# Attention of block 1: units that take the heads of both partition halves, with alternating products

## The chip, the cores and the metric

The kernel runs on one core of a Trainium2 chip. The metric is the device time of one execution in microseconds (us), lower is better; a time is the median of several runs. Engines are named as in the profile: PE (TensorE matmuls), PEld (its weight loads), DVE (VectorE), ACT (ScalarE), POOL (GpSimd), SP (the DMA queue used most).

## What is computed

The program is two blocks of a network on 512 tokens of width 1024. Block 1 projects its normalised input to many streams, runs a windowed attention in three groups of 8 heads of width 64 on some of them and a gated recurrence on others, and merges both. Block 2 (not touched here) has more attention, a second recurrence and two layers of experts. What matters is the attention of block 1, per group with dilation 1, 4 or 16:

```
s = jnp.einsum('bnqrhd,bnkrhd->bnrhqk', qb, kh) + bias
s = jnp.where(valid[None, :, None, None], s, NEG_INF)
m = jnp.max(s, axis=-1, keepdims=True)
p = jnp.exp(s - m)
den = jnp.transpose(jnp.sum(p, axis=-1), (0, 1, 4, 2, 3))
o = jnp.einsum('bnrhqk,bnkrhd->bnqrhd', p, vh) / den[..., None]
```

Queries see keys at most 64 positions away in their group's order; blocks out of range are masked. The outputs of the three groups are then mixed by their maxima and sums.

## The kernel before

`attention1` is the second stage of block 1. It first builds Q, K and V of the three groups with `matrix`: projections as triples of matmuls in split precision (lines 102 to 104, 128x512, called the projections below), with a norm and transposes (L679) for Q and K. Into the gaps of these projections a side stream, `softmaxes`, is issued a step at a time: `side.step` runs it once after each group of 12 projections.

Q and K are kept transposed, as [128, 4, 512]: a plane m of 128 partitions holds two heads, one on partitions 0 to 63 (e = 0), one on 64 to 127 (e = 1). A unit of work `unit(ph, t, e, mp, ...)` takes 128 queries (t) and two heads, those of planes 2mp and 2mp+1 on the half e. It has three parts, separated by `yield`:

1. scores: 64-row matmuls into one PSUM bank (L732 for phase 0, which is group 0, with 192 or 256 keys; L735 for phase 1, which is groups 1 and 2, with 128 keys each), then on DVE the bias is added and the row maximum taken (L742, one per head), the maximum negated (L745), and on ACT the exponential with its sum (L747, one per head);
2. four transposes of 128x128 into another bank (L753) and a copy to SBUF, `pT` (L755, on DVE for e = 0, on ACT for e = 1);
3. four products with V (L762), 64 output columns each, into the bank `ob` that all units of one t share, on the partitions of half e. The last unit of a t copies `ob` out (L764).

```
pp = slice(64 * e, 64 * e + 64)
nc.tensor.matmul(b[...], Q[0][pp, m, sl], Kt[0][pp, m, ...], start=True, stop=True)
nc.tensor.matmul(ob[pp, m * 128:m * 128 + 128], vs[a], pT[:, 2 * j + a], start=(a == 0), stop=(a == 1))
```

So one unit's score matmuls all use the same 64 rows of the PE array, and its products with V the same 64 columns. A phase has 4 (t) x 2 (e) x 2 (mp) = 16 units. Each fp32 matmul appears in the trace as two passes (two records); a transpose as one. `Lag` holds units whose later parts are due at later steps. Phase 0 runs beside the projections of groups 1 and 2; phase 1 runs beside the first half of the output gate (`gate(0)`, 48 projections) and is then drained. After that the weights of the three groups are put together on 8 partitions (transposes L821, DVE and ACT work L824 to L839, among it a reciprocal L837), beside `gate(1)`, and spread with matmuls L844 and L845, which need the last of it.

Tiles come from pools: `s` has 6 buffers, `nm` 4, `pT` 3, and all matmul outputs share 8 PSUM banks (`bank`). The framework's scheduler decides the order in which each engine gets the instructions, from the order of issue and from what each waits for; every engine then runs its list strictly in that order.

Of the kernel before, what the change touches and what calls it, by code (L numbers as in the profile page):

```python
# [14 lines left out]
AF = mybir.ActivationFunctionType  # L15
ALU = mybir.AluOpType
# [7 lines left out]
NEG = -1.0e30  # L24
# [588 lines left out]
def attention1(k, bank, feed, proj_t, hT, oaT):  # L613
    nc, tc, I = k.nc, k.tc, k.i
    es = ExitStack()
    p = k.pool("at", 1, None, es)
    dp = k.pool("atd", 1, DRAM, es)
    T = lambda shape, name, bufs=1: p.tile(shape, F32, name=name, tag=name, bufs=bufs)
    bias = T([128, 8, 512], "bias")
    st = T([128, 4, 4, 8], "stats")  # L620
# [3 lines left out]
    T2 = lambda shape, name, bufs=1: p2.tile(shape, F32, name=name, tag=name, bufs=bufs)  # L624
# [39 lines left out]
    lag = Lag()  # L664
# [51 lines left out]
                yield  # L716
        return dst

    def unit(ph, t, e, mp, Q, Kt, V, ob):

        sl = slice(t * 128, t * 128 + 128)
        pp = slice(64 * e, 64 * e + 64)
        lo = 64 if ph == 0 and t == 0 else 0
        hi = 192 if ph == 0 and t == 3 else 256
        b = bank()
        s = T2([128, 2, 256], "s", 6)
        h0 = 4 * mp + e
        for j in range(2):
            m = 2 * mp + j
            if ph == 0:  # L730
                k0 = t * 128 - 64
                nc.tensor.matmul(b[:, j * 256 + lo:j * 256 + hi], Q[0][pp, m, sl], Kt[0][pp, m, k0 + lo:k0 + hi], start=True, stop=True)  # L732
            else:
                for g in (1, 2):
                    nc.tensor.matmul(b[:, j * 256 + g * 128 - 128:j * 256 + g * 128], Q[g][pp, m, sl], Kt[g][pp, m, sl], start=True, stop=True)  # L735
        if lo:
            nc.gpsimd.memset(s[:, :, :lo], NEG)
        if hi < 256:
            nc.gpsimd.memset(s[:, :, hi:], NEG)
        for j in range(2):  # L740
            h = h0 + 2 * j
            nc.vector.tensor_tensor_reduce(s[:, j, lo:hi], b[:, j * 256 + lo:j * 256 + hi], bias[:, h, ph * 256 + lo:ph * 256 + hi], 1.0, -3.0e38,  # L742
                                           ALU.add, ALU.max, st[:, t, ph, h:h + 1])
        nm = T2([128, 2], "nm", 4)
        nc.vector.tensor_scalar(nm, st[:, t, ph, h0:h0 + 3:2], -1.0, None, ALU.mult)  # L745
        for j in range(2):
            nc.scalar.activation(s[:, j], s[:, j], AF.Exp, bias=nm[:, j:j + 1], accum_out=st[:, t, 2 + ph, h0 + 2 * j:h0 + 2 * j + 1])  # L747
        yield
        yield
        yield  # L750
        b2 = bank()
        for a in range(4):
            nc.tensor.transpose(b2[:, a * 128:a * 128 + 128], s[:, a // 2, (a % 2) * 128:(a % 2) * 128 + 128], k.id)  # L753
        pT = T2([128, 4, 128], "pT", 3)
        (nc.scalar.copy if e else nc.vector.tensor_copy)(pT.rearrange("p a q -> p (a q)"), b2)  # L755
        yield
        for j in range(2):
            m = 2 * mp + j
            hs = slice((2 * m + e) * 64, (2 * m + e) * 64 + 64)
            vs = (V[0][:, t, hs], V[0][:, t + 1, hs]) if ph == 0 else (V[1][:, t, hs], V[2][:, t, hs])  # L760
            for a in range(2):
                nc.tensor.matmul(ob[pp, m * 128:m * 128 + 128], vs[a], pT[:, 2 * j + a], start=(a == 0), stop=(a == 1))  # L762
        if e == 1 and mp == 1:
            nc.vector.tensor_copy(pv[ph][:, :, sl], ob.rearrange("p (m q) -> p m q", m=4))  # L764

    def softmaxes(ph, Q, Kt, V):
        lag = Lag()
        for t in range(4):
            ob = bank("ob")
            for e in range(2):  # L770
                for mp in range(2):
                    lag.push(unit(ph, t, e, mp, Q, Kt, V, ob))
                    lag.tick()
                    yield
        lag.drain()

    Q, Kt, V = {}, {}, {}
# [13 lines left out]
    V[0] = run(matrix(0, 2))  # L791
    lag.drain()
    side.add(softmaxes(0, Q, Kt, V))
    for g in (1, 2):
        Q[g] = run(matrix(g, 0))
        Kt[g] = run(matrix(g, 1))
        V[g] = run(matrix(g, 2))
        side.drain()
    lag.drain()
    side.add(softmaxes(1, Q, Kt, V))  # L800
    ga = T2([128, 5, 512], "v0")[:, 0:4]

# [15 lines left out]
    for a in range(4):  # L818
        b = bank()
# [1829 lines left out]
```

## Time and profile before

| | us |
|---|---|
| median of 3 runs | 3463.92 |
| lowest and highest run | 3454.38, 3468.79 |
| the profiled execution, its own time | 3452.15 |
| its span on the core | 3450.3 |
| PE busy, share of the span | 3103.6, 90% |
| DVE busy | 1538.3, 45% |
| ACT busy | 1013.0, 29% |
| POOL busy | 975.3, 28% |

A busy PE in this profile is a PE with at least one matmul under way; matmuls overlap, so the mean duration of one is longer than the distance from one to the next, and it is the distance that costs time. Where a text below gives the price of a visit (a run of equal matmuls), it is the time from its first start to the start of what follows on PE.

### The profile page before, as it was taken

The numbers are of one execution on the slowest core, as the hardware profiler recorded it, in microseconds if no ns is written. First come the engines' busy times: TensorE is split into PE (matmuls) and PEld (weight loads), VectorE is DVE, ScalarE is ACT, GpSimd is POOL, SyncE is SP. The second block draws the span as 40 slices with busy tenths as digits, with TensorE's granted clock in tenths as the row PEclk, the third lists the DMA queues.
The fourth block names the chain that finished last, engine by engine and source line by source line (L and its number), as shares of the span: only waits on it lengthen the run. The fifth ranks groups of instructions, "written<-read, shape, count | busy, mean of one in ns | idle before, by whom it ended". The sixth has DMA issues, their size and how long they took to land.

```text
span 3450.3 us, 52389 instructions
## 1 busy us (share of the span) xinstructions
PE 3103.6 (90%) x21072; PEld 2032.6 (59%) x21072; DVE 1538.3 (45%) x3435; ACT 1013.0 (29%) x2175; POOL 975.3 (28%) x859
## 2 busy tenths in 40 slices
PE   8999999998989899979999999899768579699888
PEld 6898778886768666743333333687647467333322
DVE  3233544414378687342323334331577776332212
ACT  4333333322212454211111212222557443011000
POOL 5342434332323552410000000424646344000000
PEclk9999999999989999979999999899879779899999
DMA  4121122225257232178888884343222234799998
GB/s 145 61 74 49 62 74 70 66 68 166 93 158 203 81 101 65 49 304 339 333 341 334 333 339 166 105 140 117 80 59 71 66 96 154 311 409 409 409 409 349
DMA packets 372552, 625.94 MB, mean 181 GB/s; under 512 B 43998, under 2 KB 240525, under 8 KB 372310
## 3 DMA queue, kind: packets, MB, share of 16 engines
q1 hardware_dynamic: 367190, 603.58, 49.2%
q0 software_dynamic: 5120, 19.01, 1.5%
q8 instruction: 167, 2.74, 0.3%
q14 instruction: 75, 0.61, 0.1%
HBM read 596.61 MB, written 25.91 MB: 180 GB/s over the span
## 4 chain that ended last, share of the span: by engine, by line
PE 73%; DVE 11%; DMA 8%; ACT 4%; issue 2%; POOL 2%; SPq 1%; POOLq 0%; DVEq 0%; ACTq 0%
PE ps L102 11%; PE h L1617 10%; PE ps L103 10%; PE ps L104 10%; PE yb L1656 7%; DMA w<-in_moe_w_dram 6%; PE hc L1617 4%; PE ps L1599 2%; PE ps L926 1%; PE ob L762 1%; PE ps L2253 1%; DVE acc L1100 1%; DVE pr L2308 1%; DVE N L2309 1%; PE ob L1303 1%
## 5 line engine op out<-in xcount | busy, mean ns | idle before, releaser
L201 POOL TENSOR_TENSOR wlo<-wraw,whi 128x1024 fp32r<-128x1024 f32 (+5 forms) x219 | 426.8, 1970 | 755.2 <-ACT whi L197 736.5
L1617 PE MATMUL h<-w,xT 128*64 128x512 f32 x2048 | 462.6, 597 | 23.7 <-DMA w<-in_moe_w_dram 18.1
L1617 PEld LDWEIGHTS h<-w,xT 128*64 128x64 f32 x2048 | 141.1, 137 | 335.0 <-issue 253.9
L1656 PE MATMUL yb<-w,hT 128*64 128x512 f32 (+1 forms) x1536 | 301.0, 599 | 17.8 <-ACT hT L1640 15.4
L197 ACT CAST whi<-wraw 128x2048 fp32r<-128x2048 f32 (+4 forms) x108 | 161.5, 1495 | 235.7 <-PE ps L103 111.8
L1477 POOL DMA_INDIRECT xs<-xh,ii x20 | 21.3, 1067 | 728.9 <-DVE sl L1480 708.6
L1625 DVE SCALAR_TENSOR_TENSOR th<-th,h 128x512 f32<-128x512 f32 x32 | 22.0, 688 | 413.3 <-ACT th L1624 413.3
L1656 PEld LDWEIGHTS yb<-w,hT 128*64 128x64 f32 (+1 forms) x1536 | 87.2, 128 | 197.3 <-issue 153.6
L102 PE MATMUL ps<-hT,whi 128*128 128x512 f32 x416 | 171.2, 412 | 0.0
L102 PE MATMUL ps<-whi,hT 128*128 128x512 f32 (+1 forms) x424 | 164.3, 388 | 4.9 <-DVE hT L316 2.7
L103 PE MATMUL ps<-hT,wlo 128*128 128x512 f32 x416 | 166.3, 400 | 0.0
L1624 ACT ACTIVATE th<-h 128x512 f32<-128x512 f32 x32 | 19.1, 597 | 499.7 <-PE h L1617 499.7
L104 PE MATMUL ps<-hT,whi 128*128 128x512 f32 x416 | 165.7, 398 | 0.0
L103 PE MATMUL ps<-whi,hT 128*128 128x512 f32 (+1 forms) x424 | 156.4, 369 | 0.0
L104 PE MATMUL ps<-wlo,hT 128*128 128x512 f32 (+1 forms) x424 | 154.5, 367 | 0.0
L115 POOL TENSOR_TENSOR rs<-rs_t,mhalf 128x8 f32<-128x8 f32 (+3 forms) x78 | 94.7, 1218 | 113.5 <-DVE rs_t L110 93.7
L1617 PE MATMUL hc<-w,xT 128*32 128x512 f32 x1024 | 124.2, 598 | 0.0
L1669 DVE TENSOR_TENSOR ys<-yb,g 64x512 f32<-64x512 f32 x64 | 44.1, 688 | 177.5 <-PE yb L1656 177.0
L102 PEld LDWEIGHTS ps<-whi,hT 128*128 128x128 f32 x424 | 104.3, 246 | 14.5 <-DVE hT L316 3.2
L103 PEld LDWEIGHTS ps<-whi,hT 128*128 128x128 f32 x424 | 104.6, 247 | 6.4 <-issue 1.9
L1100 DVE SCALAR_TENSOR_TENSOR acc<-glu,w,acc 128x798 f32<-128x798 f32 x90 | 106.6, 1221 | 1.0
L104 PEld LDWEIGHTS ps<-wlo,hT 128*128 128x128 f32 x424 | 103.9, 246 | 5.2 <-issue 0.2
(810 smaller groups left out, 6831.4 us busy)
## 6 DMA issues: line engine op xcount, KB each, us to landing
w<-in_moe_w_dram SPq DMA_DIRECT2D x376, 1024.0 KB
wraw<-in_w_in_dram SPq DMA_DIRECT2D x48, 1024.0 KB
aw<-in_ada_w_dram SPq DMA_DIRECT2D x192, 256.0 KB
wraw<-in_od_w_in_dram SPq DMA_DIRECT2D x27, 512.0 KB
rows<-rw_rows SPq DMA_DIRECT2D x48, 192.0 KB
w<-in_moe_w_dram POOLq DMA_DIRECT2D x8, 1024.0 KB, 10.0
xh<-xn SPq DMA_DIRECT2D x10, 512.0 KB
wraw<-in_w_proj_b_dram SPq DMA_DIRECT2D x4, 1024.0 KB
```

The source lines that it names most:

```text
L102: nc.tensor.matmul(out, L[0], R[0], start=start, stop=False)
L103: nc.tensor.matmul(out, L[1], R[0], start=False, stop=False)
L104: nc.tensor.matmul(out, L[0], R[1], start=False, stop=stop)
L115: nc.gpsimd.tensor_tensor(out, t, mh.to_broadcast(list(ss.shape)), op=ALU.pow)
L197: nc.scalar.copy(hi, raw)
L201: eng.tensor_tensor(lo[:, a:b], raw[:, a:b], hi[:, a:b].bitcast(F32), op=ALU.subtract)
L762: nc.tensor.matmul(ob[pp, m * 128:m * 128 + 128], vs[a], pT[:, 2 * j + a], start=(a == 0), stop=(a == 1))
L1100: v.scalar_tensor_tensor(acc[:, c], glu[:, c, j:j + W], w2[:, j, c:c + 1], acc[:, c], ALU.mult, ALU.add)
L1599: nc.tensor.matmul(b, back, y[:, hs], start=(i == 0), stop=(i == len(terms) - 1))
L1617: nc.tensor.matmul(bb[o:o + cap], lhs, w[:, kk % 2, fh * 512:fh * 512 + 512], start=(kk == 0), stop=(kk == 7), tile_position=(0, o))
L1656: nc.tensor.matmul(yb[o:o + cap], lhs, w[:, j, dh * 512:dh * 512 + 512], start=first, stop=last, tile_position=(0, o))
L1669: nc.vector.tensor_tensor(ys[so, ds_], yb[64 * dh:64 * dh + 64], g["gate"][so, ds_], op=ALU.mult)
```

## The change

`unit` loses its argument e and takes both halves: four heads. It has two score banks `bs`, two tiles `ss`, one tile `nm` with a column pair for each half, two `pT`, and it issues the score matmuls and the products with V alternately for e = 0 and e = 1. The bias, the maximum and the exponential still go half by half. A phase now has 8 units of two steps each in place of 16 of one; a unit has two `yield` between scores and transposes in place of three.

```
-    def unit(ph, t, e, mp, Q, Kt, V, ob):
+    def unit(ph, t, mp, Q, Kt, V, ob):
...
-        b = bank()
-        s = T2([128, 2, 256], "s", 6)
-        h0 = 4 * mp + e
+        bs = [bank() for _ in range(2)]
+        ss = [T2([128, 2, 256], "s", 6) for _ in range(2)]
         for j in range(2):
...
-                nc.tensor.matmul(b[:, j * 256 + lo:j * 256 + hi], Q[0][pp, m, sl], Kt[0][pp, m, k0 + lo:k0 + hi], start=True, stop=True)
+                for e in range(2):
+                    nc.tensor.matmul(bs[e][:, j * 256 + lo:j * 256 + hi], Q[0][pp[e], m, sl], Kt[0][pp[e], m, k0 + lo:k0 + hi], start=True, stop=True)
...
                 for g in (1, 2):
-                    nc.tensor.matmul(b[:, j * 256 + g * 128 - 128:j * 256 + g * 128], Q[g][pp, m, sl], Kt[g][pp, m, sl], start=True, stop=True)
+                    for e in range(2):
+                        nc.tensor.matmul(bs[e][:, j * 256 + g * 128 - 128:j * 256 + g * 128], Q[g][pp[e], m, sl], Kt[g][pp[e], m, sl], start=True, stop=True)
...
-        yield
-        yield
-        yield
-        b2 = bank()
-        for a in range(4):
-            nc.tensor.transpose(b2[:, a * 128:a * 128 + 128], s[:, a // 2, (a % 2) * 128:(a % 2) * 128 + 128], k.id)
+        yield
+        yield
+        pts = []
+        for e in range(2):
+            b2 = bank()
+            for a in range(4):
+                nc.tensor.transpose(b2[:, a * 128:a * 128 + 128], ss[e][:, a // 2, (a % 2) * 128:(a % 2) * 128 + 128], k.id)
...
             for a in range(2):
-                nc.tensor.matmul(ob[pp, m * 128:m * 128 + 128], vs[a], pT[:, 2 * j + a], start=(a == 0), stop=(a == 1))
+                for e in range(2):
+                    hs = slice((2 * m + e) * 64, (2 * m + e) * 64 + 64)
+                    vs = V[0][:, t + a, hs] if ph == 0 else V[1 + a][:, t, hs]
+                    nc.tensor.matmul(ob[pp[e], m * 128:m * 128 + 128], vs, pts[e][:, 2 * j + a], start=(a == 0), stop=(a == 1), skip_group_check=True)
...
-            for e in range(2):
-                for mp in range(2):
-                    lag.push(unit(ph, t, e, mp, Q, Kt, V, ob))
-                    lag.tick()
-                    yield
+            for mp in range(2):
+                lag.push(unit(ph, t, mp, Q, Kt, V, ob))
+                yield
+                lag.tick()
+                yield
```

In the changed file the scores stand on L732 and L736, bias and maximum on L746, the negation on L748, the exponential on L750, the transposes on L757, the copy on L759, the products with V on L768, the copy of `ob` on L770.

The order on PE in phase 0, at the last products with V of the first query tile, before (L102 to L104 are projections, `ps` with a number is one PSUM bank's tile, `s` the exponentials of one half of a unit):

```order
L679 MATMUL ps_1057<-cc_58,qn_971 128x128 x4
L732 MATMUL ps_1073<-qk_472,qk_273 128x256 x2
L102 MATMUL ps_832<-whi_833,hT0_90 128x512
L103 MATMUL ps_832<-whi_833,hT1_91 128x512
L762 MATMUL ob_852<-pT_1043,v0_669 64x128 x4
L753 MATMUL ps_1088<-cc_58,s_982 128x128 x4
L104 MATMUL ps_832<-wlo_834,hT0_90 128x512
```

The first products with V of the same query tile in the changed kernel:

```order
L104 MATMUL ps_830<-wlo_834,hT0_90 128x512
L768 MATMUL ob_852<-pT_936,v0_669 64x128
L768 MATMUL ob_852<-pT_943,v0_669 64x128
L768 MATMUL ob_852<-pT_936,v0_669 64x128
L768 MATMUL ob_852<-pT_943,v0_669 64x128
L768 MATMUL ob_852<-pT_936,v0_669 64x128
L768 MATMUL ob_852<-pT_943,v0_669 64x128
L768 MATMUL ob_852<-pT_936,v0_669 64x128
L768 MATMUL ob_852<-pT_943,v0_669 64x128
L757 MATMUL ps_1024<-cc_58,s_900 128x128 x4
L757 MATMUL ps_1031<-cc_58,s_901 128x128 x4
```

Four products with V of one half have become eight that change the half each time (`pT_936` is e = 0, `pT_943` is e = 1), and the transposes come eight at a time.

The order on PE in phase 1, at the fifth unit's scores, before (a unit's four scores go into one tile):

```order
L753 MATMUL ps_2215<-cc_58,s_2163 128x128 x4
L735 MATMUL ps_2226<-qk_1144,qk_828 128x128
L735 MATMUL ps_2226<-qk_1824,qk_1657 128x128
L735 MATMUL ps_2226<-qk_1144,qk_828 128x128
L735 MATMUL ps_2226<-qk_1824,qk_1657 128x128
L753 MATMUL ps_2242<-cc_58,s_2178 128x128 x4
```

and in the changed kernel, at the fourth unit:

```order
L768 MATMUL ob_2138<-pT_2199,v1_1487 64x128
L757 MATMUL ps_2246<-cc_58,s_2170 128x128 x4
L757 MATMUL ps_2253<-cc_58,s_2171 128x128 x4
L736 MATMUL ps_2263<-qk_1136,qk_828 128x128
L768 MATMUL ob_2138<-pT_2206,v1_1487 64x128
L768 MATMUL ob_2138<-pT_2199,v2_1995 64x128
L768 MATMUL ob_2138<-pT_2206,v2_1995 64x128
L768 MATMUL ob_2138<-pT_2199,v1_1487 64x128
L768 MATMUL ob_2138<-pT_2206,v1_1487 64x128
L768 MATMUL ob_2138<-pT_2199,v2_1995 64x128
L768 MATMUL ob_2138<-pT_2206,v2_1995 64x128
L736 MATMUL ps_2264<-qk_1136,qk_828 128x128
```

Here the scheduler has split visits: the first of eight products with V stands alone, ahead of transposes, and the first score ahead of the other seven. Over both phases the list of PE has 16 visits of L732, 26 of L735 and 32 of L762 before; it has 10 of L732, 11 of L736 and 26 of L768 (6 with all eight, 10 with one and 10 with seven) after. The visits of the transposes fall from 38 to 25, the stretches of projections between them from 54 to 48.

The order on DVE in the last unit of phase 1, before:

```order
L742 ISA s,stats<-ps,bias 128x256
L742 ISA stats 128x1
L742 ISA s,stats<-ps,bias 128x256
L742 ISA stats 128x1
L745 TENSOR_SCALAR nm<-stats 128x2
L755 COPY pT<-ps 128x512
```

and in the changed kernel:

```order
L746 ISA s,stats<-ps,bias 128x256
L746 ISA stats 128x1
L746 ISA s,stats<-ps,bias 128x256
L746 ISA stats 128x1
L746 ISA s,stats<-ps,bias 128x256
L746 ISA stats 128x1
L746 ISA s,stats<-ps,bias 128x256
L746 ISA stats 128x1
L748 TENSOR_SCALAR nm<-stats 128x2 x2
L759 COPY pT<-ps 128x512
```

Both negated maxima now come after all four sums with the bias, so the first exponential of a unit is released after the fourth of these instead of after the second.

## Rows read from the trace of the kernel before

**Rows 1.** The page: busy time of the engines, and the chain by engine.
```profile
PE 3103.6 (90%) x21072; PEld 2032.6 (59%) x21072; DVE 1538.3 (45%) x3435; ACT 1013.0 (29%) x2175; POOL 975.3 (28%) x859
...
PE 73%; DVE 11%; DMA 8%; ACT 4%; issue 2%; POOL 2%; SPq 1%; POOLq 0%; DVEq 0%; ACTq 0%
```

**Rows 2.** Two stretches, phase 0 and phase 1: busy us of each engine.
```profile
core 0: us, PE busy (x) PEld busy (x) DVE busy (x) ACT busy (x) POOL busy (x), PEclk, DMA share, GB/s
109.22:296.41 187.19, 187.19 (x889) 172.18 (x889) 58.62 (x140) 66.06 (x124) 82.65 (x44) 1.00 0.20 64
296.41:368.40 71.99, 70.58 (x432) 54.58 (x431) 39.76 (x108) 28.34 (x80) 10.18 (x5) 1.00 0.14 45
```

**Rows 3.** The chain of waits between 100 and 400 us: start, us, what.
```profile
109.22 0.84 PE ps L732 x4
...
128.13 1.06 PE ps L732 x4
...
300.91 1.09 PE ps L735 x8
...
304.59 0.86 PE ps L735 x6
...
308.77 0.59 PE ps L753 x4
...
312.70 0.64 PE ps L735 x4
313.34 1.02 PE ob L762 x8
...
352.83 1.64 PE ps L821 x15
...
368.47 1.05 PE ps L844 x2
```

**Rows 4.** Groups of instructions between 60 and 420 us, on ACT, DVE and PE.
```profile
L747 ACT ACTIVATE s<-s,nm 128x256 f32<-128x256 f32 x64 | 32.0, 502 | 40.6 <-DVE nm L745 40.6
...
L742 DVE CUSTOM_DVE_ANT_0 s<-ps,bias 128x256 f32<-128x256 f32 x48 | 18.4, 421 | 48.1 <-PE ps L735 29.7 <-PE ps L732 18.3
...
L762 PE MATMUL ob<-pT,v 128*64 128x128 f32 x256 | 34.8, 279 | 1.4 <-DVE pT L755 1.4
```

**Rows 5.** Timeline of PE in phase 1: start, us, engine, line.
```profile
298.97 0.39 PE L103 MATMUL ps<-hT,wlo 128*128 128x512 f32 x1
299.21 0.40 PE L104 MATMUL ps<-hT,whi 128*128 128x512 f32 x1
299.53 0.49 PE L735 MATMUL ps<-qk 64*128 64x128 f32 x2
299.95 0.50 PE L102 MATMUL ps<-hT,whi 128*128 128x512 f32 x1
300.28 0.40 PE L103 MATMUL ps<-hT,wlo 128*128 128x512 f32 x1
```

**Rows 6.** Timeline of PE in block 2's first attention, whose L1303 alternates column halves.
```profile
1199.81 0.65 PE L1303 MATMUL ob<-pT,v 128*64 128x128 f32 x6
1200.39 0.70 PE L1267 MATMUL ps<-kT,qT 96*128 96x256 f32 x2
...
1209.14 1.53 PE L1303 MATMUL ob<-pT,v 128*64 128x128 f32 x24
1210.61 0.44 PE L1287 MATMUL ps<-cc,s 128*128 128x128 f32 x2
```

**Rows 7.** Timeline of PE in the recurrence of block 1, whose L546 changes row quarter each time.
```profile
466.90 0.73 PE L546 MATMUL u<-v,kt 32*128 32x128 f32 x16
467.56 0.50 PE L102 MATMUL ps<-hT,whi 128*128 128x512 f32 x1
```

**Rows 8.** Timeline of DVE at the end of the attention.
```profile
358.99 0.68 DVE L836 TENSOR_TENSOR qn<-qn 8x512 f32<-8x512 f32 x1
361.52 0.69 DVE L764 COPY pv<-ob 128x512 f32<-128x512 f32 x1 [1.85 <-PE ob L762]
362.13 3.33 DVE L837 RECIPROCAL qn<-qn 8x512 f32<-8x512 f32 x1
...
366.53 0.67 DVE L839 SCALAR_TENSOR_TENSOR qn<-qn 8x512 f32<-8x512 f32 x1
```

**Rows 9.** Waits between 100 and 370 us: who for whom, us in total, times, longest.
```profile
POOL s L739 <- PE ps L753: 13.5, 2, 9.1
```

**Rows 10.** Stretches after the attention: PEclk is the granted clock.
```profile
370.00:380.00 10.00, 10.00 (x18) 4.33 (x17) 8.28 (x10) 0.89 (x1) 9.03 (x6) 0.64 0.31 104
380.00:390.00 10.00, 10.00 (x39) 7.94 (x37) 2.60 (x3) 0.59 (x1) 4.36 (x7) 0.85 0.00 1
```

**Rows 11.** The page, DMA on the chain by line, among the largest parts.
```profile
PE ps L102 11%; PE h L1617 10%; PE ps L103 10%; PE ps L104 10%; PE yb L1656 7%; DMA w<-in_moe_w_dram 6%; PE hc L1617 4%; PE ps L1599 2%; PE ps L926 1%; PE ob L762 1%; PE ps L2253 1%; DVE acc L1100 1%; DVE pr L2308 1%; DVE N L2309 1%; PE ob L1303 1%
```

More of the change, by code (lines that the diff above doesn't have):

```diff
@@ L717, in matrix @@
         return dst
-    def unit(ph, t, e, mp, Q, Kt, V, ob):
+    def unit(ph, t, mp, Q, Kt, V, ob):
         sl = slice(t * 128, t * 128 + 128)
-        pp = slice(64 * e, 64 * e + 64)
+        pp = [slice(64 * e, 64 * e + 64) for e in range(2)]
         lo = 64 if ph == 0 and t == 0 else 0
         hi = 192 if ph == 0 and t == 3 else 256
-        b = bank()
-        s = T2([128, 2, 256], "s", 6)
-        h0 = 4 * mp + e
+        bs = [bank() for _ in range(2)]
+        ss = [T2([128, 2, 256], "s", 6) for _ in range(2)]
         for j in range(2):
@@ L736, in unit @@
[L736 to L745, printed above, removed]
@@ L746, in unit @@
-        for j in range(2):
-            nc.scalar.activation(s[:, j], s[:, j], AF.Exp, bias=nm[:, j:j + 1], accum_out=st[:, t, 2 + ph, h0 + 2 * j:h0 + 2 * j + 1])
+                    for e in range(2):
+                        nc.tensor.matmul(bs[e][:, j * 256 + g * 128 - 128:j * 256 + g * 128], Q[g][pp[e], m, sl], Kt[g][pp[e], m, sl], start=True, stop=True)
+        nm = T2([128, 2, 2], "nm", 4)
+        for e in range(2):
+            s, b, h0 = ss[e], bs[e], 4 * mp + e
+            if lo:
+                nc.gpsimd.memset(s[:, :, :lo], NEG)
+            if hi < 256:
+                nc.gpsimd.memset(s[:, :, hi:], NEG)
+            for j in range(2):
+                h = h0 + 2 * j
+                nc.vector.tensor_tensor_reduce(s[:, j, lo:hi], b[:, j * 256 + lo:j * 256 + hi], bias[:, h, ph * 256 + lo:ph * 256 + hi], 1.0, -3.0e38,
+                                               ALU.add, ALU.max, st[:, t, ph, h:h + 1])
+            nc.vector.tensor_scalar(nm[:, e], st[:, t, ph, h0:h0 + 3:2], -1.0, None, ALU.mult)
+            for j in range(2):
+                nc.scalar.activation(s[:, j], s[:, j], AF.Exp, bias=nm[:, e, j:j + 1], accum_out=st[:, t, 2 + ph, h0 + 2 * j:h0 + 2 * j + 1])
@@ L748, in unit @@
         yield
         yield
-        yield
-        b2 = bank()
-        for a in range(4):
-            nc.tensor.transpose(b2[:, a * 128:a * 128 + 128], s[:, a // 2, (a % 2) * 128:(a % 2) * 128 + 128], k.id)
-        pT = T2([128, 4, 128], "pT", 3)
-        (nc.scalar.copy if e else nc.vector.tensor_copy)(pT.rearrange("p a q -> p (a q)"), b2)
+        pts = []
[3 more added lines that the diff above has]
+                nc.tensor.transpose(b2[:, a * 128:a * 128 + 128], ss[e][:, a // 2, (a % 2) * 128:(a % 2) * 128 + 128], k.id)
+            pT = T2([128, 4, 128], "pT", 3)
+            (nc.scalar.copy if e else nc.vector.tensor_copy)(pT.rearrange("p a q -> p (a q)"), b2)
+            pts.append(pT)
@@ L758, in unit @@
             m = 2 * mp + j
-            hs = slice((2 * m + e) * 64, (2 * m + e) * 64 + 64)
-            vs = (V[0][:, t, hs], V[0][:, t + 1, hs]) if ph == 0 else (V[1][:, t, hs], V[2][:, t, hs])
             for a in range(2):
-                nc.tensor.matmul(ob[pp, m * 128:m * 128 + 128], vs[a], pT[:, 2 * j + a], start=(a == 0), stop=(a == 1))
-        if e == 1 and mp == 1:
+                for e in range(2):
+                    hs = slice((2 * m + e) * 64, (2 * m + e) * 64 + 64)
+                    vs = V[0][:, t + a, hs] if ph == 0 else V[1 + a][:, t, hs]
+                    nc.tensor.matmul(ob[pp[e], m * 128:m * 128 + 128], vs, pts[e][:, 2 * j + a], start=(a == 0), stop=(a == 1), skip_group_check=True)
+        if mp == 1:
             nc.vector.tensor_copy(pv[ph][:, :, sl], ob.rearrange("p (m q) -> p m q", m=4))
```

## The prediction

> **What bounds the kernel now.** I read the page first: PE is busy for 90% of the span and holds 73% of the chain of waits [rows 1]. The change touches two stretches only, so I cut them out: phase 0 from its first score to the first of phase 1, 187.19 us, and phase 1 from there to the first spreading matmul L844, 71.99 us. In the first PE is never idle, in the second for 1.4 us, while DVE, ACT and POOL are busy for between 14% and 55% [rows 2]. The chain of waits confirms it: between 100 and 400 us nearly every piece of it is PE, and the visits of L732, L735 and L762 stand there with the time to the next start [rows 3]. The one wait that PE has inside is for the copy pT, 1.4 us [rows 4]. So a microsecond of PE work removed here is a microsecond of the program, as long as no new wait takes its place.
>
> **What a visit costs when one tile of the array is used.** The four-pass visits of L732 take 0.84 us (192 keys) and 1.06 us (256 keys); L735 takes 0.64 us with 4 passes, 0.86 with 6 and 1.09 with 8; L762 takes 1.02 with 8 [rows 3]. The differences for L735 give 0.11 us a pass and a fixed 0.2 us a visit (0.64 less 4 x 0.11). With the same 0.2 a pass of L762 takes 0.82 / 8 = 0.102, and L735 with 2 passes takes 0.42 [rows 5].
>
> **What it costs when the tiles alternate.** The trace has the products with V in the changed form already: L1303, also 64 output columns of 128 rows, 128 columns moving, fp32, both halves of one bank in turn. Its 24-pass visit takes 1.47 us [rows 6]; its short visit is 8 passes by the code (two key tiles, two heads, two passes; 6 are recorded) and takes 0.58 us. That is (1.47 - 0.58) / 16 = 0.055 us a pass, half of L762's, plus 0.14. For two 64-row halves with 128 or more columns there is no row. The nearest one is L546, which takes 16 passes of 32 rows and 128 columns in 0.66 us and moves to another row quarter each time [rows 7]; less 0.2 that is 0.029 a pass, about a quarter of 0.11. The bounds for two halves are therefore no overlap (0.11) and full overlap (0.055); less than 0.055 is excluded, since each half must still take its own passes one behind the other. I take 0.055: four row tiles side by side cost a quarter, so two should cost half.
>
> **The parts of the change**, by the visits that the built order shows.
> 1. Products with V. Before: 32 visits x 1.02 = 32.6 us. After: 6 whole visits (16 passes) x 1.02, 10 of a lone matmul (2 passes, priced as the 0.42 of L735) and 10 of seven (14 passes, 0.14 + 0.77 = 0.91): 6.1 + 4.2 + 9.1 = 19.4. Saved 13.2.
> 2. Scores of phase 0. Before: 8 x 0.84 + 8 x 1.06 = 15.2. After: four visits of 256 keys at 1.06, two whole ones of 192 at 0.84, and two units cut in pieces (3 and 1, 0.84 + 0.52; 2 and 2, 0.52 + 0.52): 8.3. Saved 6.9.
> 3. Scores of phase 1. Before: 128 passes x 0.11 + 26 visits x 0.2 = 19.3. After: five whole visits at 1.09 (eight passes deep on each half) and three units cut in seven and one, 1.09 + 0.42: 10.0. Saved 9.3, of which I count 8.8, since the first visits merge in the trace.
> 4. Fewer changes of form around them. Four transposes take 0.59 us ahead of a tiled form [rows 3], and sixteen transposes of the same shape run at 1.64 / 15 = 0.11 each, so about 0.15 is the change; 13 visits fewer make 2.0. The projections stand 0.24 apart, 0.32 where a tiled form follows, and 0.33 for the first after one [rows 5]; with 6 stretches fewer that is 6 x 0.18 = 1.1. Saved 3.1.
> 5. The new lag. Two score banks and two transposed banks are held at once, and both negated maxima come behind all four sums with the bias. From the last score to the first transpose a unit then needs four sums at about 0.35 us from start to start (0.42 is one's length [rows 4]), two negations, and four exponentials at 0.50 [rows 4]: about 1.8 + 2.1 = 3.9 us, where half a unit needed about 2. In phase 0 twelve projections of 0.24 lie between steps, which is cover enough (five to eight microseconds of PE work between scores and transposes of one unit). In phase 1 the middle units have 5 to 6 us of other PE work there, but the last one has only three projections and the products and transposes of the unit before it, some 3.7 us. I count 2 us lost in all; with no cover at all in the last two units it would be 5, with full cover 0. Everything queued behind those transposes on PE would wait too, and then L821.
> 6. DVE, ACT and POOL do the same number of instructions, and no DMA moves. What is late next is the DVE chain to L844: before, its last L839 ends at 367.2 and L844 starts at 368.47 [rows 3, 8], so it has about 1 us to spare, and it contains a wait of 1.85 us for the last L762. In the new order the reciprocal stands ahead of that copy, and 48 projections less those used still lie between, so I count nothing, at most 1 us if the cover is short. On POOL the four fills of masked columns keep their place ahead of a unit's sums; two of them waited 13.5 us for a buffer of `s` [rows 9], with splits of weights queued behind, and that reached PE nowhere in phase 0, where PE is never idle [rows 2].
>
> Sum: 13.2 + 6.9 + 8.8 + 3.1 - 2 = 30.0 us. Against the profiled execution, 3452.15, that makes 3422. That execution lies 11.8 us under the median of the runs shown, 3463.92, so for a median I forecast **3434 us**, 0.9% less. A measurement of this kernel can tell about 0.5%, 17 us, from no change.
>
> [...]
>
> **The rivals.**
> A. *The matmuls alternate, but do not overlap.* Then only the fixed parts go: products with V 256 x 0.102 + 26 x 0.2 = 31.3 (1.3 saved), scores of phase 0 about 1.2, of phase 1 15 x 0.2 = 3, changes 3.1, less 2 for waits: 7 us, 3457. Against it, [rows 6, 7] show the overlap for both kinds of tile. 4%.
> B. *Only one kind overlaps.* If the column halves do not, part 1 saves 1.3 and the sum is 18; if the row halves do not, parts 2 and 3 save 4 instead of 15.7 and the sum is again 18: 3446. For columns, L1303 speaks against it [rows 6]. [...] 3% for columns, 5% for rows.
> [...]
> D. *The gain is given back later.* DMA holds 8% of the chain, expert weights alone 6% [rows 1, 11]; if those transfers kept their times, 20 us or more of the gain would wait there: 3455. Against it: they are issued into buffers that come free as PE goes on, and so should move with it. 4%.
>
> **How the numbers follow.** Forecast 81%, A 4%, B 8%, C 3%, D 4%. Under 3446.6 (faster by over 0.5%) lies nearly all of the forecast, some 79%, and half of B: 0.83. Slower by over 0.5% is C: 0.03. The rest, A, D, half of B and the forecast's edge, is within 0.5%: 0.14. The range reaches down to 3420 (no waits, the clock's loss gone, the runs' own spread of some 7 us) and up to 3452, which takes in B and a bad day of the forecast, not A, C or D.
>
> **What would show it right or wrong.** In the changed profile, whole visits of L768 should take 1.0 us and of L736 and L732 1.1 (192 keys 0.84); if they take 1.8 to 2.0, it is A or B. The stretch from the first score to the first spreading matmul should be 229 us instead of 259, about half the gain in each phase, with PE waits on ACT before L757 of 1 to 3 us; more than 10 us of them, with a granted clock under 1 in phase 1, is C. The distance from L844's place to the end of the span should be unchanged within 6 us; if it has grown by 20, it is D. I would be wrong as a whole if the stretch shrinks by less than 17 us.

## The result and the profile after

The changed kernel takes 3432.14 us (median of 4 runs, 3428.88 to 3437.04) where the kernel before takes 3461.51 beside it (4 runs, 3454.38 to 3468.79): a ratio of 0.9916, 95% interval 0.989 to 0.9942. That is faster by 0.6% to 1.1%; 3434 was forecast. The profiled execution of the changed kernel took 3434.85, its span is 3432.6. Of the runs further down, one execution of the kernel with all scores on one half took 4481 us at a mean granted clock of 0.64 where its other five took 3438 to 3454, and its median is taken over these five.

The page of the changed kernel, engines' busy time [rows 1] and the largest parts of the chain by line [rows 11]:

```profile
PE 3083.4 (90%) x21072; PEld 2017.0 (59%) x21072; DVE 1528.3 (45%) x3435; ACT 1014.2 (30%) x2175; POOL 976.9 (28%) x859
...
PE ps L102 11%; PE h L1623 10%; PE ps L103 10%; PE ps L104 10%; PE yb L1662 7%; DMA w<-in_moe_w_dram 5%; PE hc L1623 4%; PE ps L1605 2%; PE ps L932 1%; PE ps L2259 1%; DVE pr L2314 1%; DVE acc L1106 1%; PE ob L1309 1%; DVE N L2315 1%; PE ps L1271 1%
```

The number of matmuls is the same, PE is busy for 20 us less, and the products with V have dropped off the list of the chain. Where the time went is seen in the stretches of the two phases and the two behind them (columns as in [rows 2]):

```profile
core 0: us, PE busy (x) PEld busy (x) DVE busy (x) ACT busy (x) POOL busy (x), PEclk, DMA share, GB/s
109.05:281.33 172.28, 172.28 (x892) 161.81 (x891) 52.31 (x140) 65.29 (x125) 82.71 (x44) 1.00 0.21 69
281.33:337.34 56.01, 55.84 (x433) 41.45 (x432) 34.92 (x108) 27.69 (x80) 10.17 (x5) 1.00 0.17 57
...
340.00:350.00 10.00, 10.00 (x18) 4.77 (x17) 8.33 (x10) 0.00 (x0) 10.00 (x6) 0.59 0.31 105
350.00:360.00 10.00, 10.00 (x40) 8.01 (x39) 1.47 (x2) 0.59 (x1) 3.24 (x7) 0.90 0.00 0
```

Phase 0 takes 172.3 us instead of 187.2, phase 1 56.0 instead of 72.0: 31.0 us less in all, 228.3 after 259.3. PE is idle for 0.17 us. Behind the attention the granted clock falls as before [rows 10]: 0.59 and 0.90, 5.1 us of full clock lost where before it was 5.1 too.

The chain of waits shows the price of the visits (start, us, what), to be held against [rows 3]:

```profile
109.11 0.84 PE ps L732 x6
...
117.66 0.85 PE ps L732 x8
...
125.43 1.06 PE ps L732 x8
...
129.62 1.02 PE ob L768 x16
130.64 1.02 PE ps L757 x8
...
173.13 0.84 PE ps L732 x4
...
179.21 1.02 PE ob L768 x14
...
285.10 1.09 PE ps L736 x16
...
320.04 1.18 ACT s L750 x5
...
337.34 1.05 PE ps L850 x2
```

A visit of 16 passes with V takes 1.02 us, what 8 passes took before; 16 passes of 128-key scores take 1.09, as 8 did. In a whole visit the doubled work is free to the hundredth of a microsecond. Where all passes are on one half, nothing is gained: the four at 173.13 take 0.84 as before, and since DVE takes the sums of two heads behind them and then waits for the next piece, they are the two heads of one half. One wait is new on the chain, 1.18 us at 320.04, on an exponential.

Added up from start to next start over PE's timeline, the 31.0 us are these:

| PE work of both phases, us | before | after | saved | forecast |
|---|---|---|---|---|
| products with V | 32.6 | 20.1 | 12.5 | 13.2 |
| scores of phase 0 | 15.2 | 9.0 | 6.2 | 6.9 |
| scores of phase 1 | 19.3 | 10.0 | 9.3 | 8.8 |
| projections (102 to 104) | 166.7 | 165.1 | 1.6 | part of the 3.1 |
| transposes, with the waits around them | 16.9 | 15.5 | 1.4 | rest of the 3.1, less 2 |

### The profile page after: what moved, and what is told of

It reads as the page before. It is cut to its first block, busy times and chain, and to the rows that moved or that the text cites. A ratio compares the mean times of both kernels' runs of the same rounds, so it can differ in the third digit from the quotient of the medians.

```text
span 3432.6 us, 52377 instructions
## 1 busy us (share of the span) xinstructions
PE 3083.4 (90%) x21072; PEld 2017.0 (59%) x21072; DVE 1528.3 (45%) x3435; ACT 1014.2 (30%) x2175; POOL 976.9 (28%) x859
## 4 chain that ended last, share of the span: by engine, by line
PE 73%; DVE 11%; DMA 8%; ACT 4%; issue 2%; POOL 2%; SPq 1%; DVEq 0%; ACTq 0%; POOLq 0%
PE ps L102 11%; PE h L1623 10%; PE ps L103 10%; PE ps L104 10%; PE yb L1662 7%; DMA w<-in_moe_w_dram 5%; PE hc L1623 4%; PE ps L1605 2%; PE ps L932 1%; PE ps L2259 1%; DVE pr L2314 1%; DVE acc L1106 1%; PE ob L1309 1%; DVE N L2315 1%; PE ps L1271 1%
## 5 line engine op out<-in xcount | busy, mean ns | idle before, releaser
L201 POOL TENSOR_TENSOR wlo<-wraw,whi 128x1024 fp32r<-128x1024 f32 (+5 forms) x219 | 426.0, 1967 | 734.0 <-ACT whi L197 708.9
L102 PE MATMUL ps<-hT,whi 128*128 128x512 f32 x416 | 171.2, 411 | 0.0
L102 PE MATMUL ps<-whi,hT 128*128 128x512 f32 (+1 forms) x424 | 163.3, 386 | 6.2 <-DVE hT L316 4.0
L104 PE MATMUL ps<-hT,whi 128*128 128x512 f32 x416 | 166.1, 399 | 0.0
L104 PE MATMUL ps<-wlo,hT 128*128 128x512 f32 (+1 forms) x424 | 154.2, 366 | 0.0
L102 PEld LDWEIGHTS ps<-whi,hT 128*128 128x128 f32 x424 | 104.1, 246 | 15.7 <-DVE hT L316 4.3
L104 PEld LDWEIGHTS ps<-wlo,hT 128*128 128x128 f32 x424 | 103.7, 245 | 5.4 <-issue 0.6
```

The source lines that it names most:

```text
L102: nc.tensor.matmul(out, L[0], R[0], start=start, stop=False)
L104: nc.tensor.matmul(out, L[0], R[1], start=False, stop=stop)
L201: eng.tensor_tensor(lo[:, a:b], raw[:, a:b], hi[:, a:b].bitcast(F32), op=ALU.subtract)
```

## The experiments

In all of them "the attention" is the stretch from the first score to the first spreading product, and "the rest" is from there to the end of the span. **Theory:** the time is saved because neighbouring matmuls on different halves of the array run side by side. **Rival:** it is saved because there are fewer and longer visits, with fewer changes of form; the alternation itself is nothing.

### Both kernels again

> The kernel before, once more, for a second trace of it. Theory (the gain passes on whole, and what the two traces differ by after the attention is the spread of executions): from the first spreading matmul L844 to the end of the span takes 3082 us in the first trace; another execution should lie anywhere within 10 us of it, and 259 us from the first score to L844 within 1 us. Rival (the gain is partly given back later): this distance is again 3082 within 3 us, while every kernel with the shorter attention shows 3092 to 3097.

Measured: 3464.87 us (10 runs), ratio 0.9998 (0.9985 to 1.001). The attention takes 259.3, as before, but the rest 3095.5 where the first profile of the same kernel had 3081.9. So 14 us lie between two executions of one program behind the attention, and only the attention's stretch can be compared to a microsecond.

> The changed kernel, once more. Both theories: 228 us from the first score to the first spreading matmul L850, within 1 us, and 3432 us in all. Theory (the gain passes on whole): the distance from L850 to the end, 3095 us in the first trace, differs by several us from trace to trace and overlaps with that of the kernel before. Rival (some is given back): it stays at 3092 to 3097.

Measured: 3437.15 us (4 runs), ratio 0.9923 (0.9897 to 0.995); the attention 228.2, the rest 3094.7. The gain in the stretch repeats to 0.1 us.

### Runs by half in place of alternation, in both kinds, and in one each

The loops of the products with V; those of the scores are turned in the same way:

```
-        for j in range(2):
-            m = 2 * mp + j
-            for a in range(2):
-                for e in range(2):
+        for e in range(2):
+            for j in range(2):
+                m = 2 * mp + j
+                for a in range(2):
```

> The unit keeps both halves, but scores and products with V go half by half. Theory (alternating tiles overlap; about two thirds of the gain is overlap and a third is fewer visits): an eight-matmul visit of products with V takes 1.84 us in place of 1.02, of phase 1 scores 1.98 in place of 1.09, of phase 0 scores with 256 keys 1.9 in place of 1.06; the stretch from first score to first spreading matmul is 228 + 20 = 248 us, the total 3452. Rival (larger units with fewer visits make the gain, the order within them does not matter): visits and stretch as in the changed kernel, 228 us within 3, total 3432.

Measured: 3451.32 us (10 runs), ratio 0.9966 (0.9949 to 0.9984), the attention 238.4: 10 us of the 31 are gone, where 20 were expected. The chain of waits shows why:

```profile
125.47 1.07 PE ps L732 x8
...
129.66 1.51 PE ob L767 x16
...
294.05 1.64 PE ps L735 x16
```

Eight passes on one half and then eight on the other take 1.51 and 1.64, between the 1.02 and 1.09 of alternation and the serial price; four and four (256 keys) take 1.07, no more than in turns. PE overlaps across the border of two runs. That left two readings: a look-ahead of a few passes, or a serial price lower than thought. The runs on one half and in pairs, below, decide it.

The same edit on the products with V alone (the scores still alternate):

> Only the scores alternate, the products with V go half by half. Theory: products with V cost 10 us more than in the changed kernel (10 visits of eight at 1.84 us, 10 of four at 1.02), the stretch is 238 us, the total 3442. Rival (column halves do not overlap, so their alternation is worth nothing): the stretch is 228 us as in the changed kernel.

Measured: 3443.09 us (10 runs), ratio 0.9943 (0.9923 to 0.9964), the attention 234.3 instead of 238: low for the same reason, 1.51 a visit.

And on the scores alone (the products with V still alternate):

> Only the products with V alternate, the scores go half by half. Theory (a matmul of another tile may start ahead of the last three or four passes before it, as the runs of halves showed with 1.51 and 1.64 us a visit): whole visits of phase 1 scores take 1.64 us in place of 1.09, those of 256 keys, four passes a half, 1.07 as before, products with V 1.02; with 12 split visits of products in place of 20 the stretch is 230 to 232 us. Rival (tiles overlap only where the order alternates): scores of 256 keys take 1.9, of phase 1 1.98, the stretch is 238 us.

Measured: 3439.87 us (4 runs), ratio 0.9933 (0.9917 to 0.9948), the attention 231.9, inside what the theory gave and not the rival's 238. Over the changed kernel's 228.2, runs of scores cost 3.7, runs of products with V 6.1, both together 10.2.

### All on one half: the overlap taken away, the order of issue kept

```
-  ..., Q[0][pp[e], m, sl], Kt[0][pp[e], m, k0 + lo:k0 + hi], ...
+  ..., Q[0][pp[0], m, sl], Kt[0][pp[0], m, k0 + lo:k0 + hi], ...
-  ..., Q[g][pp[e], m, sl], Kt[g][pp[e], m, sl], ...
+  ..., Q[g][pp[0], m, sl], Kt[g][pp[0], m, sl], ...
```

> Same order and banks as the changed kernel, but all score matmuls read the rows of half 0 (so both halves get the scores of half 0). Theory (the gain on scores is overlap of two row tiles): visits of 256 keys take 1.9 us in place of 1.06, of phase 1 1.98 in place of 1.09; stretch 228 + 11.5 = 240 us, total 3444 to 3448. Rival (fewer visits and alternating banks make it): visits and stretch as in the changed kernel.

Measured: 3445.52 us (5 runs), ratio 0.9949 (0.9932 to 0.9967), the attention 239.8 for the 240 expected. Its chain of waits:

```profile
118.21 1.49 PE ps L732 x8
...
126.64 1.92 PE ps L732 x8
...
131.70 1.02 PE ob L768 x16
...
291.10 1.98 PE ps L736 x16
```

The scores go to 1.92 and 1.98, the products with V stay at 1.02. PE's instructions in the attention stand in the changed kernel's order one for one, so the difference of 11.5 us is the overlap of the scores and nothing else.

With the products with V on one half as well; the copy of `ob` is then made twice, from that half:

```
-  nc.tensor.matmul(ob[pp[e], m * 128:m * 128 + 128], vs, ...
+  nc.tensor.matmul(ob[pp[0], m * 128:m * 128 + 128], vs, ...
```

> As the one before, and the products with V of both halves go to the 64 columns of half 0, one over the other; the copy of the bank is made twice from there. So no two tiles are left in the attention, only the larger units. Theory: visits of eight products with V take 1.84 us in place of 1.02; stretch 250 us, that is 9 us under the kernel before, the share of fewer visits. Rival (fewer visits are most of the gain): 235 us or less.

Measured: 3456.83 us (10 runs), ratio 0.9984 (0.9971 to 0.9996), the attention 250.0, as expected. A visit of products with V, in the chain of waits:

```profile
130.76 1.89 PE ob L768 x16
```

Here the order on PE moved too: the scheduler cuts fewer visits, 20 of products with V in place of 26. For this order the split of the 31.0 us is: **21.8 are the overlap** (250.0 - 228.2; 11.5 from the scores and 10.2 from the products with V) and **9.2 are the rest** (259.3 - 250.0). As an estimate, the changed kernel's own visits with V at the prices on one half (6 at 1.89, 10 at 1.67, 10 at 0.37) would take 31.7 us where they take 20.1, which puts the overlap at 23. Both theory and rival hold a part; the overlap is 70 to 75%. Of the rest, 1.4 us is the old wait for `pT`, gone here as well; the other 7.8 go with 42 visits of a tiled form in place of 74, about 0.24 each.

One more rival had no run of its own: that not two matmuls run side by side, but only the weight load of one half hides behind the matmul of the other. The traces speak against it. Alternation saves 0.64 us on 8 passes of 192 keys, 0.86 on 8 of 256 and 0.89 on 16 of 128. That is 0.16, 0.21 and 0.11 for each hidden pass, in proportion to the keys, while the weights loaded have the same 64 x 128 in all three. And the single records of a whole visit start in pairs, less than 0.01 us apart, with the next pair a full pass later (0.10 us for products with V, 0.21 for 256 keys); on one half they start one by one, 0.11 and 0.22 apart.

Both halves of the columns use the same 128 rows, and at 1.02 against 1.89 us they overlap.

### Which half goes first

The same in all three loops, of both scores and of the products with V:

```
-                    for e in range(2):
+                    for e in (1, 0):
```

> As the changed kernel, but each alternating pair begins with half 1, whose bank and copy come last. Theory (a lone matmul split off a visit costs 0.42 us and takes nothing off the rest, since the other half still has all its passes): 2 splits of products with V in place of 10 and 8 stretches of projections fewer save 5 us: stretch 223 us, total 3432 - 5 = 3427 to 3432. Rival (splits fill time in which PE would wait): no gain, 228 us, with as much more waiting for copies before the products.

Measured: 3449.6 us (5 runs), ratio 0.9964 (0.9951 to 0.9978), the attention 229.4 instead of 223. A miss: phase 0 gained 1.0, phase 1 lost 2.1. The loss is one wait; DVE's, POOL's and PE's timeline around it (start, us, engine, line; in brackets the idle time before):

```profile
310.04 2.09 DVE L748 TENSOR_SCALAR nm<-stats 128x2 f32<-128x2 f32 x2
...
307.37 4.66 POOL L201 TENSOR_TENSOR wlo<-wraw,whi 128x1024 fp32r<-128x1024 f32 x2 [20.51 <-ACT whi L197]
...
314.69 1.98 PE L768 MATMUL ob<-pT,v 128*64 128x128 f32 x16 [3.13 <-ACT pT L759]
```

Two negations that take 0.29 us in the changed kernel take 2.09 here, until POOL's two splits of a weight end at 312.03. The exponentials start behind them, PE is idle for 3.1 us, and the next visit takes 1.98 in place of 1.02, at a granted clock of 0.87 over 305 to 318 us. So the new chain from scores to transposes has little cover in phase 1, as the forecast feared, and a small change of order uncovers it.

The long negations are no single case. In the 13 traces together 85 of the 416 negations (L745 in the kernel before, L748 in the changed one) start while POOL runs such a split, and every one of them ends only after the split does, within 0.2 us; 63 take 0.5 to 2.4 us, where those that start beside no POOL work take 0.15 to 0.17. The changed kernel has four long ones as well, but where PE has other work.

The rest is 3107.7, 12 more than the changed kernel's. The edit also moved instructions of later stages; whether those or the clock there made the 12 us wasn't tried.

### Pairs, and a whole query tile at once

The halves change after every two matmuls (four passes), in the products with V and in the scores of phase 1; those of phase 0 have one matmul a head and keep their turns:

```
+            for e in range(2):
...
-                    for e in range(2):
...
-            for a in range(2):
-                for e in range(2):
...
+            for e in range(2):
...
+                for a in range(2):
```

> The halves change places after every two matmuls (four passes) in place of after every one, in the scores and in the products with V; everything else is the changed kernel's. Runs of eight passes a half overlapped by about three passes (visits of 1.51 and 1.64 us where strict turns take 1.02 and 1.09), runs of four passes wholly (256-key scores, 1.07). Theory, TensorE looks some three to four passes ahead of the one that runs, whichever half they belong to: runs of four hide as well as single turns, whole visits of the products with V take 1.02 to 1.10 us, of the 128-key scores 1.09 to 1.20, the attention from its first score to the first spreading product 228 to 230 us (228.2 with single turns). Rival, the 256-key case was wide enough only because its second half's weights were early, and short runs lose at each change of half: 1.2 us and more a visit, 232 to 236 us.

Measured: 3445.38 us (8 runs), ratio 0.9943 (0.9925 to 0.9962), the attention 231.3. The chain of waits:

```profile
129.99 1.07 PE ob L767 x16
...
290.54 1.19 PE ps L735 x16
292.62 0.58 PE ob L767 x4
...
294.92 1.02 PE ob L767 x12
```

The whole visits take 1.07 and 1.19, as the look-ahead gives, and not 1.2 and more throughout. The stretch is yet 1.3 us over the top of what was expected, because of the visits that the scheduler cuts: it now takes the first pair (0.58, one half alone), and the other twelve passes still take 1.02, since the other half has all its eight. Over both phases the products with V cost 22.2 instead of 20.1, two thirds of the 3 us.

The products with V of both units of a query tile in one visit, with four buffers of `pT` and five of `s`:

```
-            pT = T2([128, 4, 128], "pT", 3)
+            pT = T2([128, 4, 128], "pT", 4)
...
-        for j in range(2):
-            m = 2 * mp + j
+        if mp == 0:
+            held.append(pts)
+            return
+        pq = held + [pts]
+        for m in range(4):
```

> The products with V of both units of a query tile are issued in one visit of 16 matmuls (32 passes, 16 a half), not in two of eight; the transposed probabilities of the first unit are held until then (four buffers for them in place of three, five for scores in place of six). A visit's price is the deeper half's passes at about 0.102 us and 0.2 us once: 16 passes 1.84 us where two visits take 2.04. Theory, the price of a visit that does not depend on its work is 0.2 us and each change of form before and after it costs 0.1 to 0.2 us more: visits of 1.84 us, the attention 222 to 226 us against 228.2. Rival, with fewer buffers for scores and products that come later, TensorE waits for the probabilities of the next unit: 0.5 to 2 us for each of the eight query tiles, attention 229 to 240 us.

Measured: 3427.64 us (5 runs, 3425.47 to 3444.21), ratio 0.9916 (0.9885 to 0.9946), the attention 222.3 of the 222 to 226 expected. The chain of waits, and the line of its core with the mean granted clock:

```profile
138.44 1.90 PE ob L771 x32
...
core 0: 3423.8 us, clock 0.943
```

A visit of 32 passes takes 1.90 for two of 1.02, and the scheduler leaves fewer visits cut in two: the products with V go from 20.1 to 16.2 us. PE's stall on the exponentials at the end of phase 1 stays (fourteen of its last sixteen transposes take 2.5 us, where eight take 0.8 elsewhere in that phase), and no buffer makes a new one. With five buffers of `pT` and four of `s`:

> As the run before it, with five buffers for transposed probabilities and four for scores. If the buffers of the transposed probabilities were what held the run before back, its waits go and the attention takes 222 to 226 us; if it was those of the scores, the waits grow and it takes 3 us or more longer than the run before. If neither held it back, both take the same within 1 us.

Measured: 3436.25 us (5 runs, 3425.76 to 3443.74), ratio 0.9917 (0.9888 to 0.9945), the attention 222.3 again: neither buffer held it back. Its PE instructions stand in the same order as those of the run before, yet its profiled execution is 18 us longer, all of it in the rest, at this clock:

```profile
core 0: 3441.8 us, clock 0.936
```

This is the shortest attention found: 5.9 us less than in the changed kernel, in two executions. In the total it can't be told from it, since the intervals cover each other.

## Why the prediction was right

**What bounds the kernel.** Right. PE work taken out shortened the stretch by 31.0 us for 30.0 forecast, and the medians lie 29.4 apart, 3432 for 3434. In the total the interval of 20 to 38 us can't tell it closer. That the sum came within 1 us is partly luck: parts 1, 2 and 4 gave 2.0 us less than forecast, parts 3 and 5 gave 2.9 more.

**Parts 1 to 3, the overlap.** The price of 0.055 us a pass, taken from the alternating L1303 for column halves and from between bounds for row halves, held for both: 1.02 and 1.09 for the whole visits, where one half alone takes 1.89 and 1.98. Full overlap was the right bound. Two sizes were off, for one reason. The forecast priced a cut visit by its number of passes: 0.91 for fourteen, and 0.52 for each piece of the unit cut "2 and 2". What counts is the half with the more passes. Fourteen passes are eight on one half and six on the other, and take 1.02; "2 and 2" are four passes on one half in each piece, and take 0.84 each. That is 0.7 us in part 1, with the lone matmuls at 0.37 instead of 0.42, and 0.7 in part 2. Part 3 measured the 9.3 that was worked out; the discount to 8.8 was not needed.

**Part 4, fewer changes of form.** 3.1 was forecast. The projections, which absorb some of it, save 1.6; the transposes save 1.4 with the waits around them, and 1.4 of waits stood among them before [rows 4]. As PE still stalls at the end of phase 1, the two can't be parted to better than half a microsecond: part 4 is about 2.5. Taken by itself, all that is not overlap is the 9.2 us that the run without any overlap still saves, 1.4 of it the old wait; the forecast's rival A had 7 for it, after 2 taken off for waits.

**Part 5, the new lag.** Right in its place and mechanism, over 2 us too dear in the sum: PE's old wait for `pT` of 1.4 went, which the forecast had not counted, and a new one of about 1 came. The old one was a negation held by a split. POOL's, DVE's and PE's timelines of the kernel before:

```profile
348.13 2.35 POOL L201 TENSOR_TENSOR wlo<-wraw,whi 128x1024 fp32r<-128x1024 f32 x1 [45.26 <-ACT whi L197]
...
349.11 1.40 DVE L745 TENSOR_SCALAR nm<-stats 128x2 f32<-128x2 f32 x1
350.42 0.68 DVE L755 COPY pT<-ps 128x512 f32<-128x512 f32 x1
...
351.16 1.09 PE L762 MATMUL ob<-pT,v 128*64 128x128 f32 x8 [1.41 <-DVE pT L755]
```

The negation lasts until the split has ended at 350.48, the copy of `pT` stands behind it, and PE waits for the copy. In the changed kernel the next split starts at 319.81, behind the last negations, so most of these 1.4 us are luck and not the change. ACT's and PE's timelines of the changed kernel at the last unit, whose scores end at 316.35:

```profile
317.84 1.89 ACT L197 CAST whi<-wraw 128x2048 fp32r<-128x2048 f32 x1
319.63 0.51 ACT L750 ACTIVATE s<-s,nm 128x256 f32<-128x256 f32 x1
...
319.79 0.43 PE L768 MATMUL ob<-pT,v 128*64 128x128 f32 x2
320.28 1.42 PE L757 MATMUL ps<-cc,s 128*128 128x128 f32 x6
```

The first transposes start 3.9 us after the scores, the very figure worked out, but by another sum: the four biases and two negations end at 318.1, and then a cast of a weight on ACT, which the forecast did not know of, holds the exponentials until 319.63. The six transposes take 1.26 us, until 321.54, instead of 0.6: they wait for the exponentials. The run with the late half first shows that this cover can fail by 3 us.

**Part 6.** Right for DVE: the chain to L850 ends in time. DVE's timeline, to hold against [rows 8]:

```profile
330.78 3.34 DVE L843 RECIPROCAL qn<-qn 8x512 f32<-8x512 f32 x1
...
334.59 0.67 DVE L770 COPY pv<-ob 128x512 f32<-128x512 f32 x1
...
335.78 0.67 DVE L845 SCALAR_TENSOR_TENSOR qn<-qn 8x512 f32<-8x512 f32 x1
```

The reciprocal stands ahead of the copy, as read from the order, and the last step ends at 336.45, 0.9 us before L850.

**The clock.** The low end of the range reckons with the clock's loss behind the attention gone, and no run shows that. The loss stayed as it was: the granted clock is 0.50 over 10.2 us in both profiles, from 372.8 us before and from 341.7 in the changed kernel, 5.1 us of full clock in each.

**The rivals.** A (no overlap) and B (one kind only) fall: the runs on one half show what they would have looked like, 250.0 and 239.8. C (phase 1 unit by unit at a lower clock, and so slower) did not come: phase 1's granted clock is 1.00. That PE's waits would lower it over the whole phase was the author's assumption, and no run shows it; in the run with the late half first it is 0.87 over 305 to 318 us, around one wait, and 0.97 over the phase. D (given back later) looked true in the first pair of profiles, where the rest grew from 3081.9 to 3095.3. The second run of the kernel before has 3095.5, so it is the spread of executions. The last two kernels, with one order on PE, spread by 18 us in the rest, with the mean clock at 0.943 and 0.936; over 3424 us that difference is 24 us of full clock, enough for it. The largest part that was found lies between 1331 and 1581 us, where the granted clock is 0.90 in the one and 0.86 in the other, 10 us of full clock; why was not traced.

## What to carry to other kernels

Where matmuls use half of the array's rows or half of its columns, issue those of the two halves in turn: here a pair cost what one did, for rows (8 and 8 passes 1.09 us, as 8 alone) and columns (1.02, as 8 alone) alike, and a visit cost what its deeper half costs (8 and 6 passes 1.02). Keep such visits whole and long: without any overlap, 32 visits fewer were still worth 7.8 us here, about 0.24 each. Then look at what the paired unit waits for: twice the work stands between its scores and its transposes, and the cover for that was nearly used up here. Look also at what POOL does beside a short DVE operation in that chain: here negations of 0.15 us took up to 2.4 beside its splits.

## What the runs showed of the hardware

- PE overlaps across a border of two runs on different halves, by some three to four passes: 8 and 8 passes take 1.51 (products with V) and 1.64 us (128-key scores) where one half alone takes 1.89 and 1.98, with a pass at 0.102 and 0.11; 4 and 4 passes of 256 keys overlap wholly (1.07).
- Two matmuls on different halves start less than 0.01 us apart and cost one pass together, for row halves (0.21 us to the next pair with 256 keys) and column halves (0.10) alike; a visit costs what its deeper half costs (8 and 6 passes 1.02 us, as 8 and 8).
- A DVE negation of 128 x 2 elements that starts while POOL splits a weight (L201) ends only after the split: 85 of 85 in 13 traces, up to 2.4 us for an operation of 0.15. POOL's other work beside a negation, 41 cases, did not hold it. No run was made for this alone.
